# Two feed-forwards' gated results, turned by transposing DMAs of 16-bit words instead of TensorE transposes

## Chip, cores and metric

One core of a Trainium2 chip. The metric is the device time of one execution in microseconds (us). Engines in short: PE is TensorE, PEld its weight loads, DVE VectorE, ACT ScalarE, POOL GpSimd, SP SyncE (it issues most DMAs).

## What is computed

A decoder layer for 256 tokens of 2048 features, in float32. In the order of the program:

```
h = layer_norm(alpha * x + 0.5 * swiglu(x, w_ffn1_gu, w_ffn1_down))
h = layer_norm(alpha * h + mixers(h))          # retention and sliding-window attention, gated
h = layer_norm(alpha * h + 0.5 * swiglu(h, w_ffn2_gu, w_ffn2_down))
h = layer_norm(alpha * h + sigmoid(h @ w_ple_gate) * (p @ w_ple_proj))

def swiglu(x, w_gu, w_down):
    g, u = split(x @ w_gu, 2)                  # 2048 -> 2 x 5632
    return (silu(g) * u) @ w_down              # 5632 -> 2048
```

The change lies in `swiglu`, between the gate and the product with `w_down`, in both feed-forwards (f1 and f2).

## The kernel before

**Products.** Every float32 product is made of three faster ones: an operand is parted into a high half (rounded to fp32r, by ACT, line 98) and a low rest (by DVE, line 99), and `Sum.add` (lines 393 to 395) issues low x high, high x high and high x low into one PSUM bank. A matmul has 128 rows of tokens (two halves t = 0, 1) and up to 512 columns.

**Weights** come as chunks of 512 KB, loaded by SP (line 112) into buffers of one pool, `slots`, with 46 buffers of 4 KB per partition that all bigger tiles of the kernel share. A chunk is then parted by ACT and DVE. A plan lists all units of weights in the order in which they are used; `fill` (line 279) loads and parts units ahead of TensorE until some 45 matmuls are ready and some 90 loaded, as long as a budget of buffers allows. It is called whenever a unit is done, so the order on each engine's queue is fixed when the program is built, and every engine works through its queue in order.

There are four kinds of units. `Single` (P in the strings of line 873 ff.) is one chunk and 12 matmuls. `Folded` (F, line 147) is the same, but its low half is made by ACT (a negated copy, line 163) and an accumulating DMA that POOL issues (line 164) in place of DVE's subtraction; f1 uses four of them in a block. `Seven` (S) takes a pair of chunks and makes the four sub-products of a 2 x 2 block scheme with seven sums in place of eight; DVE makes sums of weights for it (lines 189 to 192). `Prepared` (D, f2 alone) is a Seven whose sums were made and stored earlier.

**A feed-forward** (`ffn`) goes through its 5632 columns of g and u in eleven blocks j of 512. In each, `block` (line 425) runs the units, which fill the banks `pg` and `pu` (and four more for the sevens). Then the sums are folded (lines 500 to 504, 993), ACT applies Silu (994 or 999), and DVE multiplies (995 or 1001): the result `v` has 128 tokens on the partitions, two halves of tokens and 512 features, in float32. For the second product the features must lie on the partitions, so `v` is turned: `turned(j, v)` (line 929). It takes two PSUM banks, lets TensorE transpose eight squares of 128 x 128 (line 937) and ACT copy the two banks into `raw` (line 939). `raw` is parted only when the blocks are through (`convert`, line 943), or used as it is for the sevens of the second product.

**What sets the place of the turn.** `side` is a list of jobs; behind every unit's matmuls `run_side` (line 329) takes the first one and calls it. `later(n, job)` (line 1130) puts a job behind n others. At the end of block j line 1002 asks for `later(2, turned)`, so the turn is issued behind the third unit of block j + 1, when `v` has long been ready. PSUM has eight banks, given out in turn.

The units of a block of f1 stand in the order F F S S F S S F, and each F counts two units of `run_side`, one for g and one for u.

Of the kernel before, what the change touches and what calls it, by code (L numbers as in the profile page):

```python
# [8 lines left out]
F32 = mybir.dt.float32  # L9
F32R = mybir.dt.float32r  # L10
I32 = mybir.dt.int32
AF = mybir.ActivationFunctionType
ALU = mybir.AluOpType
PSUM = bass.MemoryType.PSUM

P = 128
S = 256
# [38 lines left out]
def layer(ctx: ExitStack, tc: tile.TileContext, io):  # L56
    nc = tc.nc
    sync, act, dve, pool, pe = nc.sync, nc.scalar, nc.vector, nc.gpsimd, nc.tensor
# [8 lines left out]
    def bank(name):  # L67
        return psum.tile([P, 512], F32, tag="ps", name=name)

    def banks(name):  # L70
        return [bank(name + str(j)) for j in range(2)]

    def slot(shape, dt, name):
        return slots.tile(shape, dt, tag="slot", name=name)
# [477 lines left out]
    def rsqrt(dst, var, n, eps):  # L552
# [7 lines left out]
        )  # L560
        s = small.tile([P, n], I32, tag=f"ns{n}", name="ns", bufs=2)
        dve.tensor_scalar(s, v[:, 0].bitcast(I32), 1, None, ALU.logical_shift_right)
        y = small.tile([P, n], I32, tag=f"ny{n}", name="ny", bufs=2)
        dve.tensor_scalar(y, s, -1.0, float(0x5F3759DF - 2**31), ALU.mult, ALU.add)
# [37 lines left out]
    def ln_stats_by_root(stats, i, t, eps, between):  # L602
# [4 lines left out]
        root = small.tile([P, 1], F32, tag="nq1", name="nroot")  # L607
        act.activation(root, mv[:, 1:2], AF.Sqrt, bias=roots[eps], scale=4.0)
        v = small.tile([P, 1], F32, tag="nb1", name="nv")
# [10 lines left out]
    def table_of(f):  # L620

        act.activation(warm, warm, f)
# [16 lines left out]
    def ln_turn(y, t, i, new, k0, nk, keep=None):  # L639

        ps = bank(f"lnps{i}{t}{k0}").rearrange("p (a b) -> p a b", a=4)[:, :nk]
        for j in range(nk):
            k = k0 + j
            pe.transpose(ps[:, j, :], y[k // 4][:, t, k % 4 * P : (k % 4 + 1) * P], ident)
        if keep is not None:
            full = keep[:, k0 % 4 : k0 % 4 + nk, t * P : (t + 1) * P]
            act.copy(full, ps)
            ps = full
        dst = new[:, k0 : k0 + nk, :]
        split(dst[:, :, t * P : (t + 1) * P], dst[:, :, S + t * P : S + (t + 1) * P], ps)  # L650

    class Norm:
# [36 lines left out]
        def turn(self, t, c):  # L689

            args = self.y, t, self.i, self.new
            if c < 3 and (t, c + 1) != self.put_off:
                self.more(t, c + 1)
            self.sums_behind()
            if c == 0:
                for k0 in (0, 2):
                    ln_turn(*args, k0, 2, self.keep.get(c))
            else:
                ln_turn(*args, 4 * c, 4, self.keep.get(c))
# [19 lines left out]
        def run(self, steps, lhs, events, blks=(), calm=2):  # L719


            self.vectors = vectors.pop()
            table_of(AF.Sqrt)
            self.new = big.tile([P, KD, 512], F32R, tag="ht", name=f"ht{self.i}")
# [20 lines left out]
        def first(self, steps, lhs, sums, events):  # L745
# [14 lines left out]
            self.put_away()  # L760
            table_of(AF.Silu if self.i < 2 else AF.Sigmoid)

# [48 lines left out]
    ident = const.tile([P, P], F32, name="ident")  # L811
# [23 lines left out]
    def rotary_table(nm):  # L835

        inv, sgn = (0, 2) if nm == "r" else (1, 3)
        pos_i = slot([P, S], I32, "pos_i" + nm)
        act.dma_start(pos_i, io["positions"].broadcast_to([P, S]))
# [20 lines left out]
        yield  # L860
        act.activation(nb, n, AF.Sin)
        yield
# [5 lines left out]
        yield  # L868
        act.activation(cos, na, AF.Sin)
        yield  # L870
# [48 lines left out]
    def ffn(name, i, ht, norm, keep, residual, keepers, away):  # L919
# [3 lines left out]
        raws = []  # L923
# [4 lines left out]

        def turned(j, v):

            raw = slot([P, 4, S], F32, f"{name}a{j}")
            raws.append(raw)
            ps = banks(f"{name}t{j}")
            for k in range(4):
                for t in range(2):
                    at = slice(k % 2 * S + t * P, k % 2 * S + t * P + P)
                    pe.transpose(ps[k // 2][:, at], v[:, t, k * P : (k + 1) * P], ident)
            for h in range(2):
                act.copy(raw[:, 2 * h : 2 * h + 2], ps[h].rearrange("p (b n) -> p b n", b=2))

        acts = {}

# [5 lines left out]
        for j in range(KF // 4):  # L948
# [40 lines left out]
            if got:  # L989
                g, v = got  # L990
                for x, ps in ((g, pg), (v, pu)):
                    for t in range(2):
                        dve.tensor_tensor(x[:, t], x[:, t], ps[t], ALU.add)  # L993
                act.activation(g, g, AF.Silu)  # L994
                dve.tensor_tensor(v, g, v, ALU.mult)
            else:
                v = slot([P, 2, 512], F32, f"{name}v{j}")
                for t in range(2):
                    act.activation(v[:, t], pg[t], AF.Silu)
                for t in range(2):  # L1000
                    dve.tensor_tensor(v[:, t], v[:, t], pu[t], ALU.mult)
            later(2, lambda j=j, v=v: turned(j, v))
        stats = small.tile([P, 2, 4, 6], F32, tag="stats", name=name + "st", bufs=1)

        def others(n, ahead=45):
# [77 lines left out]
    def joined(ps, name, dst=None):  # L1083
        lo = half(name + "lo")
        v = half(name + "v") if dst is None else dst
        for f in range(2):
            act.copy(lo[:, f], ps[f][:, S:])
            dve.tensor_tensor(v[:, f], ps[f][:, :S], lo[:, f], ALU.add)
        return v
# [40 lines left out]
    def later(n, job):  # L1130
        for j in range(n):
            if len(side) <= j:
                side.append(idle)
        side.insert(n, job)
# [683 lines left out]
```

## Time and profile before

| | |
|---|---|
| median of 3 runs | 2269.6 us (2269.53 to 2271.87) |
| time of the profiled execution | 2269.44 us |
| its span, from first to last instruction | 2267.3 us |
| granted TensorE clock | 0.999 |
| matmuls and transposes on PE | 10482, 2258.9 us busy |
| DVE | 2576 instructions, 1975.9 us |
| ACT | 1543 instructions, 1272.5 us |
| DMA | 536.69 MB, mean 237 GB/s |

The span is 2 us shorter than the execution's time, which has a start and an end around it. Busy time is the union of an engine's instructions; matmuls overlap each other in the pipeline (0.39 us each, one started every 0.23 us), so PE can be busy all the time and still vary in pace. Times inside the trace are given from the start of the span. f1's blocks lie in about 10 to 478 us, f2's in about 1480 to 1945 us, the second products behind each. A row of a group gives line, engine, operation, tiles (written <- read), shapes, count, busy time and mean duration of one, and then the engine's idle time in front of them and what ended it. A row in time gives start, duration, and in square brackets the idle time just before.

### The profile page before, as it was taken

What the parts mean: (1) busy time and instruction counts of PE and PEld (TensorE: products, weight loads), DVE (VectorE), ACT (ScalarE), POOL (GpSimd) and SP (SyncE); (2) the same over time, 40 slices, a digit from 0 to 9 for tenths busy, and PEclk for the clock granted to TensorE, in tenths of its full rate; (3) what the DMA queues carried; (4) which work ended last, traced back from release to release, by engine and by line L of the source; (5) the groups of instructions that cost most, each with busy time, mean ns of one, the idle gap of its engine ahead of it and who ended that gap; (6) DMA issues with size and microseconds to landing.
All of it is one profiled execution on the core that took longest, in us unless ns stands there. A gap on an engine that the chain in (4) does not pass through costs nothing.

```text
span 2267.3 us, 29270 instructions
## 1 busy us (share of the span) xinstructions
PE 2258.9 (100%) x10482; PEld 1877.7 (83%) x10482; DVE 1975.9 (87%) x2576; ACT 1272.5 (56%) x1543; POOL 37.1 (2%) x49
## 2 busy tenths in 40 slices
PE   9999999999999999999999999999999999999998
PEld 7888888888888888888778888888888888888887
DVE  7988989999989887888789788689999999889887
ACT  6676776656555444535566454455555565555543
POOL 0000010000000000000000000000000000000000
PEclk9999999999999999999999999999999999999999
DMA  9888898865677878775456568787867766555772
GB/s 316 249 261 252 238 262 243 250 208 186 216 285 261 291 282 289 256 236 183 140 158 225 183 211 293 271 288 247 297 242 250 255 197 218 196 190 209 290 269 73
DMA packets 216889, 536.69 MB, mean 237 GB/s; under 512 B 17052, under 2 KB 21532, under 8 KB 216744
## 3 DMA queue, kind: packets, MB, share of 16 engines
q1 hardware_dynamic: 209000, 511.28, 65.9%
q0 software_dynamic: 5760, 20.97, 5.1%
q10 hardware_dynamic: 1984, 2.58, 0.4%
q8 instruction: 82, 1.34, 0.2%
q14 instruction: 63, 0.52, 0.1%
HBM read 484.43 MB, written 29.36 MB: 227 GB/s over the span
## 4 chain that ended last, share of the span: by engine, by line
PE 78%; DVE 1%; DMA 1%; ACT 0%; issue 0%; ACTq 0%; DVEq 0%
PE f2g L395 3%; PE f2g L393 3%; PE f2g L394 3%; PE rqk L344 3%; PE f2u L393 2%; PE f2u L395 2%; PE f2u L394 2%; PE aqk L344 2%; PE f1d L395 2%; PE f2d L394 2%; PE f2d L395 2%; PE f1d L393 2%; PE f1d L394 2%; PE f2d L393 2%; PE f1e L395 1%; PE f2e L394 1%
## 5 line engine op out<-in xcount | busy, mean ns | idle before, releaser
L99 DVE TENSOR_TENSOR lf_gu<-rf_gu,hf_gu 128x1024 fp32r<-128x1024 f32 (+1 forms) x229 | 271.9, 1210 | 11.1 <-ACT hf_gu L98 10.4
L98 ACT CAST hf_gu<-rf_gu 128x1024 fp32r<-128x1024 f32 (+1 forms) x229 | 232.8, 1041 | 30.2 <-DMA rf_gu<-in_f_gu 29.9
L99 DVE TENSOR_TENSOR lf_down<-rf_down,hf_down 128x1024 fp32r<-128x1024 f32 x150 | 178.8, 1220 | 19.0 <-ACT hf_down L98 18.5
L99 DVE TENSOR_TENSOR lw_in_f<-rw_in_f,hw_in_f 128x1024 fp32r<-128x1024 f32 x140 | 167.5, 1220 | 25.0 <-ACT hw_in_f L98 24.7
L98 ACT CAST hf_down<-rf_down 128x1024 fp32r<-128x1024 f32 x150 | 151.7, 1049 | 50.7 <-DMA rf_down<-in_f_down 18.0
L98 ACT CAST huf_gu<-uf_gu 128x1024 fp32r<-128x1024 f32 x75 | 79.0, 1053 | 147.5 <-DVE uf_gu L190 138.0
L98 ACT CAST hw_in_f<-rw_in_f 128x1024 fp32r<-128x1024 f32 x140 | 140.3, 1050 | 3.2 <-PE rv L394 1.4
L98 ACT CAST hvf_gu<-vf_gu 128x1024 fp32r<-128x1024 f32 x75 | 79.1, 1055 | 31.7 <-DVE vf_gu L192 30.8
L99 DVE TENSOR_TENSOR luf_gu<-uf_gu,huf_gu 128x1024 fp32r<-128x1024 f32 x75 | 91.4, 1219 | 0.0
L99 DVE TENSOR_TENSOR lvf_gu<-vf_gu,hvf_gu 128x1024 fp32r<-128x1024 f32 x75 | 91.4, 1218 | 0.0
L393 PE MATMUL f1g<-hf_gu,xt 128*128 128x512 f32 x232 | 90.6, 390 | 0.2 <-ACT hf_gu L98 0.2
L395 PE MATMUL f1g<-lf_gu,xt 128*128 128x512 f32 x232 | 90.7, 391 | 0.0
L394 PE MATMUL f1g<-hf_gu,xt 128*128 128x512 f32 x232 | 90.4, 390 | 0.0
L393 PE MATMUL f2g<-hf_gu,ht 128*128 128x512 f32 x217 | 84.7, 390 | 0.0
L395 PE MATMUL f2g<-lf_gu,ht 128*128 128x512 f32 x217 | 84.7, 390 | 0.0
L394 PE MATMUL f2g<-hf_gu,ht 128*128 128x512 f32 x217 | 84.5, 390 | 0.0
L994 ACT ACTIVATE eve<-eve 128x1024 f32<-128x1024 f32 x20 | 21.2, 1061 | 100.4 <-DVE eve L993 100.4
L395 PE MATMUL f1u<-lf_gu,xt 128*128 128x512 f32 x192 | 75.0, 390 | 0.7 <-DMA lf_gu<-rf_gu 0.7
L393 PE MATMUL f1u<-hf_gu,xt 128*128 128x512 f32 x192 | 75.7, 394 | 0.0
L394 PE MATMUL f1u<-hf_gu,xt 128*128 128x512 f32 x192 | 74.9, 390 | 0.0
L393 PE MATMUL f2u<-hf_gu,ht 128*128 128x512 f32 x172 | 68.2, 397 | 0.0
L395 PE MATMUL f2u<-lf_gu,ht 128*128 128x512 f32 x172 | 67.1, 390 | 0.0
(1468 smaller groups left out, 6734.7 us busy)
## 6 DMA issues: line engine op xcount, KB each, us to landing
rf_gu<-in_f_gu SPq DMA_DIRECT2D x360, 512.0 KB
rf_down<-in_f_down SPq DMA_DIRECT2D x176, 512.0 KB
rw_in_f<-in_w_in_f SPq DMA_DIRECT2D x148, 512.0 KB
lf_gu<-rf_gu POOLq DMA_DIRECT2D x40, 512.0 KB, 7.0
rw_rv<-in_w_rv SPq DMA_DIRECT2D x32, 512.0 KB
rw_ret<-in_w_ret SPq DMA_DIRECT2D x32, 512.0 KB
rw_mix<-in_w_mix SPq DMA_DIRECT2D x32, 512.0 KB
rw_pg<-in_w_pg SPq DMA_DIRECT2D x32, 512.0 KB
```

The source lines that it names most:

```text
L98: act.copy(dst_hi, src)
L99: (lo_engine or dve).tensor_tensor(dst_lo, src, dst_hi, ALU.subtract)
L344: pe.matmul(ps[f], hi[:, kk, f * P : (f + 1) * P], rhs(k), start=k == 0, stop=k == n_k - 1,)
L393: pe.matmul(o, al, bh, start=first, stop=False)
L394: pe.matmul(o, ah, bh, start=False, stop=False)
L395: pe.matmul(o, ah, bl, start=False, stop=self.left == 0)
L994: act.activation(g, g, AF.Silu)
```

## The change

`turned` no longer uses TensorE or PSUM. ACT copies the 16-bit words of `v` apart, all lower ones and all upper ones (`words`); one DMA on SP's queue transposes the sixteen squares of 128 x 128 words into `moved`; ACT copies these into `raw`, each word to its place. A float32 is thus moved as two words, bit for bit. `words` and `moved` are two buffers of the pool. The three steps are issued at different places: the copies apart behind the second unit of the next block (`later(1, ...)`), the DMA behind the third (`later(0, turn)`), the copies together behind the sixth (`later(3, joined)`).

```diff
+U16 = mybir.dt.uint16
...
         def turned(j, v):
-            raw = slot([P, 4, S], F32, f"{name}a{j}")
-            raws.append(raw)
-            ps = banks(f"{name}t{j}")
-            for k in range(4):
-                for t in range(2):
-                    at = slice(k % 2 * S + t * P, k % 2 * S + t * P + P)
-                    pe.transpose(ps[k // 2][:, at], v[:, t, k * P : (k + 1) * P], ident)
+            words = slot([P, 2, 2, 512], U16, f"{name}w{j}")
+            of_v = v.bitcast(U16).rearrange("p t (n h) -> p h t n", h=2)
             for h in range(2):
-                act.copy(raw[:, 2 * h : 2 * h + 2], ps[h].rearrange("p (b n) -> p b n", b=2))
+                act.copy(words[:, h], of_v[:, h])
+            moved = slot([P, 2, 2, 4, P], U16, f"{name}m{j}")
+
+            def turn():
+                sync.dma_start_transpose(
+                    moved.rearrange("p h t k n -> p (h t k) n"), words.rearrange("p h t n -> p (h t n)")
+                )
+
+            def joined():
+                raw = slot([P, 4, S], F32, f"{name}a{j}")
+                raws.append(raw)
+                of_raw = raw.bitcast(U16).rearrange("p k (t n h) -> p h t k n", t=2, h=2)
+                for h in range(2):
+                    act.copy(of_raw[:, h], moved[:, h])
+
+            later(0, turn)
+            later(3, joined)
...
-            later(2, lambda j=j, v=v: turned(j, v))
+            later(1, lambda j=j, v=v: turned(j, v))
```

In the built program PE has 176 transposes fewer, ACT 44 copies of 128 x 1024 words each way in place of 44 of 128 x 512 out of PSUM, and SP 22 DMAs more. The order of everything else is the same, but the buffers that tiles get are other ones, and with them what some loads wait for.

## Prediction

> **What bounds the kernel now.** I read the page first, then the waits of TensorE, then the busy time by stretch, and at last the order in time around one of the 22 places where the change cuts.
>
> ```profile
> span 2267.3 us, 29270 instructions
> ...
> PE 2258.9 (100%) x10482; PEld 1877.7 (83%) x10482; DVE 1975.9 (87%) x2576; ACT 1272.5 (56%) x1543; POOL 37.1 (2%) x49
> ...
> q1 hardware_dynamic: 209000, 511.28, 65.9%
> q0 software_dynamic: 5760, 20.97, 5.1%
> q10 hardware_dynamic: 1984, 2.58, 0.4%
> ```
>
> ```profile
> PE warm L1697 <- POOL ident masks.py:199: 1.4, 1, 1.4
> PE f1u L395 <- DMA lf_gu<-rf_gu: 0.7, 1, 0.7
> ```
>
> TensorE is busy for the whole span, and the longest things it ever waited for are 1.4 us at the start and, once, 0.7 us for an accumulating DMA of the first feed-forward. A busy PE could still be a slow one, so the cadence matters:
>
> ```profile
> 99.20 0.39 PE L394 MATMUL f1g<-hf_gu,xt 128*128 128x512 f32 x1
> 99.42 0.40 PE L395 MATMUL f1g<-lf_gu,xt 128*128 128x512 f32 x1
> 99.66 1.04 PE L937 MATMUL f1t<-ident,evw 128*128 128x128 f32 x8
> 100.45 0.48 PE L393 MATMUL f1u<-hf_gu,xt 128*128 128x512 f32 x1
> 100.77 0.40 PE L394 MATMUL f1u<-hf_gu,xt 128*128 128x512 f32 x1
> 101.00 0.39 PE L395 MATMUL f1u<-lf_gu,xt 128*128 128x512 f32 x1
> ```
>
> Matmuls start every 0.23 us (100.77 to 101.00), one behind the other. So the kernel is bound by the number of TensorE instructions, and whatever leaves TensorE without making it wait is gained in full. The second question is how much room the others have:
>
> ```profile
> 91.50:133.20 41.70, 41.70 (x189) 34.64 (x188) 37.53 (x46) 28.47 (x33) 3.47 (x4) 1.00 0.84 250
> 133.20:174.90 41.70, 41.70 (x189) 34.64 (x188) 37.60 (x46) 28.50 (x33) 3.44 (x4) 1.00 0.85 247
> 1520.00:1945.00 425.00, 425.00 (x1921) 353.11 (x1920) 400.01 (x470) 241.03 (x279) 0.00 (x0) 1.00 0.71 241
> ```
>
> The first two rows are blocks j = 2 and 3 of the first feed-forward (f1), the third the eleven blocks of the second (f2), 38.6 us each. Behind the length stand PE, PEld, DVE, ACT, POOL, the granted clock, the DMA share and GB/s. DVE has 4.1 us free in a block of f1, ACT 13.2, the DMA engines 15% or 6.3 us. In f2 the DMA engines have 29%, 11.2 us a block.
>
> **The change part by part.**
>
> *TensorE loses 176 transposes.*
>
> ```profile
> L937 PE MATMUL f1t<-ident,evw x80: 271/273/273, 99.7 to 476.9; 128*128 128x128 f32 x80
> L937 PE MATMUL f2t<-ident,evw x80: 271/273/273, 1568.7 to 1942.0; 128*128 128x128 f32 x80
> L937 PE MATMUL f1t<-ident,f1v x8: 271/272/273, 58.0 to 58.7; 128*128 128x128 f32 x8
> L937 PE MATMUL f2t<-ident,f2v x8: 270/273/273, 1527.6 to 1528.4; 128*128 128x128 f32 x8
> ```
>
> That is 22 groups of eight. From the matmul at 99.42 to the second one behind the group at 100.77 it is 1.35 us; without the group it is two steps of 0.227, 0.45 us. A group costs 0.90 us, 22 of them **19.7 us**. All of it is on the path, since TensorE never rests.
>
> *ScalarE: two copies out, four in.*
>
> ```profile
> L939 ACT COPY f1a<-f1t x22: 572/586/592, 61.1 to 477.2; 128x512 f32<-128x512 f32 x22
> L939 ACT COPY f2a<-f2t x22: 573/587/596, 1528.3 to 1942.4; 128x512 f32<-128x512 f32 x22
> ```
>
> ```profile
> L98 ACT CAST hf_gu<-rf_gu 128x1024 fp32r<-128x1024 f32 x61 | 63.8, 1045 | 0.0
> ```
>
> The four new copies move 1024 two-byte words per partition, each with a stride of two words on one side. No row has such a form. They might take 0.5 us (twice as fast for half the bytes) or 2.1 us (twice as slow for the stride); I take the cast's 1.05 us, the nearest row of the same count. Per turn ACT gains 4 x 1.05 - 2 x 0.59 = 3.0 us, and 28.5 becomes 31.5 us of a block of 41 us. Whether that is hidden depends on the place:
>
> ```profile
> 96.40 1.06 ACT L98 CAST hvf_gu<-vf_gu 128x1024 fp32r<-128x1024 f32 x1 [0.40 <-DVE vf_gu L192]
> 97.36 1.04 ACT L98 CAST hf_gu<-rf_gu 128x1024 fp32r<-128x1024 f32 x1
> 101.67 1.06 ACT L98 CAST huf_gu<-uf_gu 128x1024 fp32r<-128x1024 f32 x1 [2.75 <-DVE uf_gu L190]
> 104.02 1.07 ACT L939 COPY f1a<-f1t 128x512 f32<-128x512 f32 x2
> 110.86 1.05 ACT L98 CAST hvf_gu<-vf_gu 128x1024 fp32r<-128x1024 f32 x1 [0.38 <-DVE vf_gu L192]
> 111.82 1.05 ACT L98 CAST hf_gu<-rf_gu 128x1024 fp32r<-128x1024 f32 x1
> 116.08 1.06 ACT L98 CAST huf_gu<-uf_gu 128x1024 fp32r<-128x1024 f32 x1 [2.69 <-DVE uf_gu L190]
> ```
>
> In the built order the two parting copies come behind the first of these casts, at 97.4, and end at 99.5. The casts behind them slide into the 2.75 us that ACT idled before 101.67. The two joining copies come behind the cast that ends at 111.9 and fill the 2.69 us idle before 116.08. In between, the two copies at 104.02 go. So ACT's additions cost nothing, and what follows 104.02 is one microsecond earlier. If the stride doubles the price, parting ends at 101.6 and the next cast at 102.7; DVE wants it at 102.95, so even that about fits.
>
> *SP: one more issue, and a wait.* The transposing DMA stands in the built order of SP behind the load that was issued at 89.21. It waits for the parting copies, 99.5.
>
> ```profile
> 89.21 1.61 SPq L112 DMA_DIRECT2D rf_gu<-in_f_gu  x2
> 94.18 0.88 SPq L112 DMA_DIRECT2D rf_gu<-in_f_gu  x2
> 103.46 0.37 SPq L112 DMA_DIRECT2D rf_gu<-in_f_gu  x1
> ```
>
> ```profile
> 114.75 0.69 DVE L189 TENSOR_TENSOR uf_gu<-rf_gu,rf_gu 128x512 f32<-128x512 f32 x1
> ```
>
> Queued behind it are the second load of the first row, which went out before 91, and the two from 94.18; the next one left at 103.46 anyway. They lose up to 9 us. The first two are wanted by ACT at 111.82 (with the joining copies, 113.9) and by DVE at 114.75. Issued from 99.5 on, behind a transposition that takes T, and needing some 5 us to land (the accumulating DMAs of the same size, below, needed 4.9 at least), they are in time while T stays under about 9 us. ACT reaches the joining copies at 111.9, so there the DMA itself may last 12.4 us from 99.5. Past that, ACT stands still with the casts of all weights behind it. The accumulating DMAs, whose results TensorE reads, are the tightest spot:
>
> ```profile
> 108.36 0.86 POOL L164 DMA_DIRECT2D lf_gu<-rf_gu  x1 [21.47 <-PE f1g L395]
> ```
>
> ```profile
> 115.97 0.40 PE L395 MATMUL f1u<-lf_gu,xt 128*128 128x512 f32 x1
> ```
>
> ```profile
> DMA to landing us min/median/max: 4.9/6.6/10.3
> ```
>
> Issued at 108.36 and used at 115.97: 7.6 us for something that takes 6.6 in the middle and 10.3 at worst. This one is issued 1 us earlier (104.02 above) and used 0.9 us earlier, a draw. The last one of a block is not issued earlier but used 0.9 us earlier; the one wait of 0.7 us in the table says that some have no slack. I put 3 us in all for f1: 0.9 us at two or three blocks, the rest for transfers that now run beside the transposition.
>
> *The DMA itself.* No transposing DMA is in this trace, so its engine time has to be bounded. 512 KB moved as a weight load: 65.9% of 16 engines for 511 MB is 0.659 x 2267.3 x 0.524 / 511.28 = 1.5 us. The accumulating DMA, also from SBUF to SBUF: 0.051 x 2267.3 / 40 = 2.9 us. By packets: q1's take 0.659 x 16 x 2267.3 us / 209000 = 114 ns for 2446 bytes on average, q10's 73 ns for 1300, so roughly 26 ns a packet and 0.036 ns a byte. In pieces of 256 bytes (128 two-byte words of a row) it would be 2048 x 35 / 16 = 4.5 us, in pieces of 32 bytes 16384 x 27 / 16 = 28 us. Less than the load's 1.5 has no reason. I take 3 to 4.5 us, next to the one row that is SBUF to SBUF; that is inside the 6.3 us free in f1 and far inside f2's 11.2.
>
> The page "DMA: Bandwidth & Descriptors" of the Trainium skill (Latency and other measured facts) gives 261 GB/s for a transposing DMA, an estimated 2.0 us for this one; the sum would stay the same. No run here shows it.
>
> *What is nowhere on the path.* Two PSUM banks a block fall away; no wait of TensorE in the list above is for a bank. The words and the moved words take two more buffers, for some 15 us each; loads that wait for a buffer may shift by a few us, which I leave in the range.
>
> **Sum.** 2269.4 (the profiled execution's own time; the median of the three runs is 2269.6, so nothing to correct) - 19.7 + 3 = **2253 us**, 0.7% faster. What this measurement can tell from no change is about 0.2%, 4.5 us.
>
> **The rivals.**
>
> *The pieces are small (slower).* The place is the DMA engines in f1; it decides from 6.3 us of engine time per transposition, and with f2's 9.9 us gain to lose, the total turns slower from about 7.2. Between 4.5 and 28 I take the middle by ratio, 11.2 us: f1 then lasts 11 x (11.2 - 6.3) = 54 us longer than now, f2 just fits and keeps its 9.9, 2269.4 + 54 - 9.9 = 2313 us. At 28 us it would be 2269.4 + 11 x 21.7 + 11 x 16.8 = 2693. For it: two-byte elements, and a share of 0.84 already. Against it: nothing that the trace shows.
>
> *The blocks go one after another (slower).* The DMA holds sixteen squares of 128 x 128 words. If each were issued like a load (0.44 us, by the two in 0.88 us above) that is 7 us, if each ran its course alone (4.9 us) 78. The middle by ratio is 23 us; ACT is then stuck for 23 - 12.4 in each of 22 turns, 2269.4 - 19.7 + 233 = 2483 us. The Trainium skill, "VectorE: DVE Perf Modes" (The three transpose paths), gives 1309 ns for one such square by DMA against 390 ns on TensorE. Sixteen in a row are an estimated 20.9 us, and this sum would be 2437. On TensorE this trace has 273 ns, and 99 ns from one to the next, so the page's figures for squares taken singly need not hold in a row.
>
> *The accumulating DMAs eat f1's gain.* Their slack is near nothing, and every block moves 0.5 MB more. f1 stays as it is, f2 gains: 2259.5 us.
>
> *DVE takes over.* 37.5 of 41.7 us are busy, and the chain of a block begins with TensorE's last sums:
>
> ```profile
> 125.33 0.69 DVE L501 TENSOR_TENSOR evw<-eve,f12s 128x512 f32<-128x512 f32 x1 [1.50 <-PE f12s L395]
> 130.02 1.37 DVE L993 TENSOR_TENSOR eve<-eve,f1g 128x512 f32<-128x512 f32 x2 [0.75 <-PE f1g L395]
> 132.74 1.37 DVE L993 TENSOR_TENSOR evw<-evw,f1u 128x512 f32<-128x512 f32 x2 [1.35 <-PE f1u L395]
> ```
>
> But its idle time, 1.50 + 0.75 + 1.35, is all waiting for TensorE and more than 0.9. If DVE were the bound after all, nothing would be gained: 2268.
>
> **How the numbers follow.** Forecast 0.50 (its own range 2248 to 2260), f1's gain lost 0.10, DVE 0.06, small pieces 0.25, one after another 0.09. The range begins at 2247, under the full 19.7 (2249.7) by what two banks fewer may give. To leave out no more than 0.2 it must take in the cheaper 0.15 of the small pieces, to 2330. Faster by over 0.2%: 0.50 + 0.10 = 0.60. Within: 0.06 and 0.01 of the small pieces, 0.07. Slower: 0.33.
>
> **What would show it.** The L937 groups gone and TensorE's steps of 0.23 us unbroken through the place, its waits still under a few us, blocks of f1 of 40.8 us: right. TensorE waiting for lf_gu by DMA in every block of f1: the accumulating DMAs. ACT idle before the joining copies with a DMA as releaser, or SP idle behind the transposing DMA: one of the slow rivals, told apart by the DMA share in f1 (towards 1.0 for small pieces, unchanged for blocks one after another). The time from issue to landing of the transposing DMA decides everything: under 9 us the forecast stands.

## The result, and the profile after

| | before | after |
|---|---|---|
| median | 2269.84 us (6 runs) | 2261.84 us (6 runs, 2261.55 to 2263.47) |
| ratio, 95% interval | | 0.9965 [0.9953, 0.9977] |
| profiled execution, its span | 2269.44, 2267.3 us | 2261.55, 2259.8 us |

The kernel is 8.0 us faster. The forecast was 16.4 us (2253): the direction came out right, but a little under half of the gain came. The stated range, 2247 to 2330, holds the measured time; it was that wide for the sake of the slow rivals. Line numbers of the changed kernel are one higher than before (matmuls 394 to 396, casts 99, subtractions 100, loads 113, accumulating DMAs 165); the parting copies are line 936, the transposing DMA 940, the joining copies 949.

The page of the changed kernel, first lines and DMA part:

```profile
span 2259.8 us, 29055 instructions
...
PE 2244.9 (99%) x10306; PEld 1856.8 (82%) x10306; DVE 1975.7 (87%) x2576; ACT 1345.9 (60%) x1587; POOL 37.1 (2%) x49
...
DMA packets 262649, 548.22 MB, mean 243 GB/s; under 512 B 62812, under 2 KB 67292, under 8 KB 262504
...
q1 hardware_dynamic: 254760, 522.82, 68.5%
```

The 176 transposes are gone (10482 to 10306). PE is busy 14.0 us less, but the span shrank by only 7.5: what PE stands idle grew from 8.4 to 14.9 us. A matmul's record lasts 0.39 us and the next one starts 0.23 us behind it, so a delay of up to some 0.16 us (an estimate from these two) leaves no idle time; the waits listed below can therefore be less than what was lost. Before, 17052 packets were under 512 bytes; now 45760 more are, 2080 for each of 22 transpositions, which for 512 KB are pieces of 256 bytes.

The new operations (line, engine, operation, tiles, count: shortest/median/longest ns, first and last start):

```profile
L936 ACT COPY f2w<-evw x20: 1036/1042/1048, 1558.9 to 1933.6; 128x1024 uint16<-128x1024 uint16 x20
...
L949 ACT COPY f1a<-f1m x22: 1342/1352/1366, 69.4 to 481.6; 128x1024 uint16<-128x1024 uint16 x22
L949 ACT COPY f2a<-f2m x22: 1333/1352/1368, 1535.3 to 1944.6; 128x1024 uint16<-128x1024 uint16 x22
...
L940 SPq DMA_TRANSPOSE f1m<-f1w x11: 1323/1920/3397, 56.9 to 468.7; - x11
L940 SPq DMA_TRANSPOSE f2m<-f2w x11: 1323/1894/3316, 1520.4 to 1934.7; - x11
```

Parting costs 1.04 us a copy, joining 1.35, and SP's issue 1.3 to 3.4 us.

**Where the time came from.** Three stages can be dated by the first matmul of the product behind each: `rv`, the first product behind f1; `f2g`, the first of f2; `pg`, the first behind f2. First and last start stand behind the durations. Before:

```profile
L393 PE MATMUL rv<-hw_rv,ht x128: 388/390/478, 706.2 to 884.3; 128*128 128x512 f32 x128
L393 PE MATMUL f2g<-hf_gu,ht x217: 388/390/482, 1473.1 to 1929.7; 128*128 128x512 f32 x109
L393 PE MATMUL pg<-hw_pg,ht x128: 388/390/481, 2165.4 to 2254.7; 128*128 128x512 f32 x128
```

After:

```profile
L394 PE MATMUL rv<-hw_rv,ht x128: 389/389/478, 699.8 to 877.9; 128*128 128x512 f32 x128
L394 PE MATMUL f2g<-hf_gu,ht x217: 387/389/478, 1466.5 to 1922.2; 128*128 128x512 f32 x109
L394 PE MATMUL pg<-hw_pg,ht x128: 389/389/499, 2157.3 to 2247.1; 128*128 128x512 f32 x128
```

Eleven turns of 0.90 us are 9.9 us in each feed-forward. f1 gained 706.2 - 699.8 = **6.4 us**. f2, from `f2g` to `pg`, took 692.3 us and now takes 690.8: **1.5 us**. So f1 loses 3.5 of its 9.9, and f2 8.4. These two numbers, "f1 gain" and "f2 gain", are given for every experiment below, each from its own three rows. They come from one profiled execution. Six kernels of this study run f1 as the changed kernel does, and gained 6.4, 7.6, 6.3, 7.2, 6.1 and 7.2 us there: a single value is good to about 0.8 us. This is the scatter between kernels that have the same turn in f1; between kernels with other copies or buffers there it may be larger.

**Who waits now.** TensorE's longest waits (us in total, times, longest):

```profile
PE f1u L396 <- DMA lf_gu<-rf_gu: 2.9, 5, 1.0
PE warm L1710 <- POOL ident masks.py:199: 1.4, 1, 1.4
PE f26s L396 <- DVE luf_gu L100: 0.8, 1, 0.8
PE f28s L396 <- DVE luf_gu L100: 0.8, 1, 0.8
PE f27s L396 <- DVE luf_gu L100: 0.8, 1, 0.8
PE f25s L396 <- DVE luf_gu L100: 0.5, 1, 0.5
```

In f1 it is the accumulating DMAs, 2.9 us where it was 0.7. In f2, where TensorE had not waited once, there are now twelve rows, 4.5 us in all. The four longest are shown: in the blocks 5 to 8 it waits for `luf_gu`, the low half of a sum of weights that DVE makes for the sevens. That is also where f2's loss lies. If a block's stretch ends with the last matmul of its sevens, the stretches were, in us, and behind the comma DVE's busy time in them:

| stretch of block | 2, 3, 4, each | 5 | 6 | 7 | 8 | 5 to 8 |
|---|---|---|---|---|---|---|
| before | 41.0 | 41.1, 38.1 | 41.7, 40.3 | 41.0, 36.5 | 41.7, 41.1 | 165.5 |
| the change | 40.1 to 40.2 | 41.3, 35.6 | 42.9, 42.3 | 42.1, 35.9 | 42.8, 42.2 | 169.1 |
| no_dma (below) | 40.1 to 40.2 | 40.1, 36.0 | 42.7, 42.2 | 40.1, 38.9 | 40.8, 40.2 | 163.7 |
| far_f2 (below) | 40.1 to 40.2 | 40.2, 36.5 | 42.2, 41.6 | 40.1, 38.8 | 40.8, 40.1 | 163.3 |

The blocks 2 to 4 gain 0.8 to 0.9 us each. The blocks 5 to 8 should gain 3.6 and lose 3.6, 7.2 of the 8.4 us. The profile's rows of these four (columns as in the prediction):

```profile
1665.70:1707.00 41.30, 40.65 (x178) 33.05 (x177) 35.56 (x43) 24.55 (x28) 0.00 (x0) 1.00 0.82 285
1707.00:1749.90 42.90, 41.71 (x182) 33.60 (x181) 42.31 (x50) 30.21 (x34) 0.00 (x0) 1.00 0.79 250
1749.90:1792.00 42.10, 40.99 (x179) 32.99 (x178) 35.91 (x44) 23.09 (x27) 0.00 (x0) 1.00 0.75 262
1792.00:1834.80 42.80, 41.62 (x181) 33.51 (x180) 42.21 (x50) 30.13 (x34) 0.00 (x0) 1.00 0.79 244
```

In the stretches 5 and 7 DVE stands idle for 5.7 and 6.2 us; in 6 and 8 it is busy all but 0.6 us, and the block goes at DVE's pace. So what DVE misses in one block TensorE waits for in the next. Without the DMA (no_dma) that is left once: 4.1 us idle in stretch 5, 0.5 in 6.

One long stretch of each feed-forward, f1 and then f2:

```profile
100.00:470.00 370.00, 366.95 (x1612) 301.81 (x1611) 339.39 (x407) 286.69 (x305) 29.56 (x35) 1.00 0.93 264
1515.00:1930.00 415.00, 410.69 (x1797) 335.97 (x1796) 392.21 (x461) 266.57 (x291) 0.00 (x0) 1.00 0.76 251
```

DVE is busy 392 of 415 us in f2, so it has little to make up for what it receives late. And SP, f1 at the place that the prediction looked at, in order of time:

```profile
87.73 2.90 SPq L113 DMA_DIRECT2D rf_gu<-in_f_gu  x2
98.14 1.91 SPq L940 DMA_TRANSPOSE f1m<-f1w  x1
100.15 7.67 SPq L113 DMA_DIRECT2D rf_gu<-in_f_gu  x5
```

For 7.5 us (90.63 to 98.14) nothing was issued, and then five loads follow in a row. SP's waits ahead of the transposing DMA in f2:

```profile
SPq L940 <- ACT hf_gu L99: 34.9, 3, 15.5
SPq L940 <- ACT bf_gu L99: 34.6, 6, 8.9
SPq L940 <- PE f2g L395: 14.4, 3, 8.7
SPq L940 <- PE f2u L396: 8.1, 1, 8.1
```

ScalarE as the releaser (by the casts close behind the parting copies) is read as the wait for the words (wait_only, below, names them); TensorE is the wait for a buffer, as SP has it in front of its loads too.

### The profile page after: what moved, and what is told of

Same layout as the page of the kernel before. It is cut to its first block, busy times and chain, and to the rows that moved or that the text cites. A ratio compares the mean times of both kernels' runs of the same rounds, so it can differ in the third digit from the quotient of the medians.

```text
span 2259.8 us, 29055 instructions
## 1 busy us (share of the span) xinstructions
PE 2244.9 (99%) x10306; PEld 1856.8 (82%) x10306; DVE 1975.7 (87%) x2576; ACT 1345.9 (60%) x1587; POOL 37.1 (2%) x49
## 3 DMA queue, kind: packets, MB, share of 16 engines
q1 hardware_dynamic: 254760, 522.82, 68.5%
## 4 chain that ended last, share of the span: by engine, by line
PE 89%; DVE 4%; DMA 4%; issue 3%; ACT 0%; ACTq 0%; POOL 0%; POOLq 0%; DVEq 0%
PE rqk L345 3%; PE f2g L396 2%; PE f2g L395 2%; PE f2g L394 2%; PE f1g L394 2%; PE f1g L396 2%; PE f1g L395 2%; PE f1u L396 2%; PE f2u L396 2%; PE f2u L395 2%; PE f2u L394 2%; DMA lf_gu<-rf_gu 2%; PE f1u L394 2%; PE f1u L395 2%; PE aqk L345 2%
## 5 line engine op out<-in xcount | busy, mean ns | idle before, releaser
L100 DVE TENSOR_TENSOR lf_down<-rf_down,hf_down 128x1024 fp32r<-128x1024 f32 x150 | 178.8, 1219 | 19.7 <-ACT hf_down L99 17.5
```

What stands on the lines that cost most here:

```text
L100: (lo_engine or dve).tensor_tensor(dst_lo, src, dst_hi, ALU.subtract)
```

## The experiments

The theory after the result: the transposition itself is quick and ScalarE's copies are hidden, but the transposing DMA on SP's queue makes weight loads late, by its wait, its traffic or its buffers, and in f2 DVE passes that on to TensorE. Rivals: ScalarE's copies delay the casts; or the transposes were hidden in part and there was never more to gain. In the expectations L is late loads, C ScalarE's copies and B the two buffers; from wait_only to reuse the letters are new: A is SP's wait, B the traffic, C the extra buffer. All ratios are against the kernel before on the same chip; its medians there lie between 2269.5 and 2270.3 us, so that a difference between runs of two chips holds up to 0.8 us of that; "lf_gu" is TensorE's total wait for accumulating DMAs in f1 (0.7 before).

| run | median us | ratio, 95% interval | f1 gain | f2 gain | lf_gu |
|---|---|---|---|---|---|
| the change | 2261.84 | 0.9965 [0.9953, 0.9977] | 6.4 | 1.5 | 2.9 |
| no_turn | 2255.24 | 0.9941 [0.9927, 0.9954] | 5.8 | 8.1 | 4.0 |
| only_f1 | 2262.02 | 0.9967 [0.9954, 0.9979] | 7.6 | 0.1 | 1.6 |
| only_f2 | 2268.94 | 0.9994 [0.9986, 1.0003] | -0.7 | 0.7 | 0.8 |
| act_queue | 2300.61 | 1.0139 [1.0125, 1.0152] | -25.7 | -4.7 | 25.0 |
| late_turn | 2265.82 | 0.9981 [0.9973, 0.999] | 3.8 | 0.0 | 3.7 |
| no_dma | 2253.28 | 0.9923 [0.991, 0.9937] | 9.7 | 7.1 | 0.7 |
| no_join | 2261.5 | 0.996 [0.9947, 0.9972] | 3.7 | 3.6 | 4.3 |
| two_less | 2267.26 | 0.9986 [0.9977, 0.9995] | 6.3 | -3.4 | 3.1 |
| wait_only | 2259.49 | 0.9954 [0.9942, 0.9967] | 4.1 | 5.8 | 4.9 |
| traffic_only | 2255.44 | 0.9936 [0.9923, 0.995] | 9.2 | 4.9 | 1.4 |
| plain_copy | 2257.84 | 0.9945 [0.9932, 0.9957] | 8.2 | 3.9 | 1.3 |
| reuse | 2264.67 | 0.9976 [0.9967, 0.9986] | 3.8 | 0.6 | 4.7 |
| late_both | 2273.77 | 1.0015 [1.0007, 1.0024] | -4.1 | 1.4 | 12.1 |
| late_both3 | 2269.06 | 1.0 [0.9992, 1.0009] | 0.1 | 4.0 | 6.0 |
| late_far | 2265.84 | 0.9983 [0.9972, 0.9993] | -15.3 | 7.8 | 17.8 |
| far_f2 | 2255.27 | 0.9937 [0.9923, 0.9951] | 7.2 | 8.1 | 2.4 |
| far_f2_8 | 2255.57 | 0.9938 [0.9925, 0.9951] | 6.1 | 6.2 | 3.0 |
| far_room34 | 2253.37 | 0.9928 [0.9914, 0.9942] | 7.2 | 9.2 | 2.7 |

### Which half loses, and how much there was to gain

**no_turn**, against the kernel before (features are not turned):

```diff
-            ps = banks(f"{name}t{j}")
...
-                    pe.transpose(ps[k // 2][:, at], v[:, t, k * P : (k + 1) * P], ident)
...
-                act.copy(raw[:, 2 * h : 2 * h + 2], ps[h].rearrange("p (b n) -> p b n", b=2))
+                act.copy(raw[:, 2 * h : 2 * h + 2], v[:, h].rearrange("p (b n) -> p b n", b=2))
```

> Nothing is turned at all: the transposes are gone and ACT copies v into raw as it stands, so the feed-forwards multiply the wrong numbers; it shows what TensorE's 176 transposes cost when nothing takes their place. If each group of eight is worth its 0.90 us everywhere: 2269.8 - 19.7 = 2250 us, f2 faster by 9.9. If VectorE bounds f2's blocks whatever the turn costs: f2 gains some 2 to 4 us, in all 2256 to 2258 us, with TensorE waiting for VectorE's luf and lvf in f2 as in the changed kernel.

**only_f1** and **only_f2**: one feed-forward by DMA, the other by TensorE as before.

```diff
-            later(1, lambda j=j, v=v: turned(j, v))
+            if name == "f1":
+                later(1, lambda j=j, v=v: turned_dma(j, v))
+            else:
+                later(2, lambda j=j, v=v: turned_pe(j, v))
```

> The first feed-forward turns by DMA, the second on TensorE as before. The traces of before and after, matmul by matmul, put 6.1 us of the gain into f1's blocks and 1.9 into f2's. If the two are independent: 2263.5 us. If f1's DMA turns hurt something later (buffers shifted for the rest of the program): slower than that.

> The second feed-forward turns by DMA, the first on TensorE. Independent: 2268 us, with TensorE's waits for luf and lvf in f2's blocks 5 to 8 as in the changed kernel. If the buffers left over from f1 had caused the waits in f2: 2260 us, f2's full 9.9 us.

Measured: no_turn 2255.24, so 14.8 us are there when nothing is transposed, between the two times expected. It does not reach 19.7: f2 gains 8.1 of 9.9, and f1 only 5.8, with 4.0 us of waits for accumulating DMAs although nothing is transposed. That the missing part was never there to gain is ruled out for f1 by no_dma below (9.7). only_f1 gains what the whole change gains, only_f2 nothing that can be told from zero. The greater loss is f2's.

### ScalarE's copies

**no_dma** parts and joins in the same places, but nothing is moved between:

```diff
-            moved = slot([P, 2, 2, 4, P], U16, f"{name}m{j}")
-            def turn():
-                sync.dma_start_transpose(
...
-                    act.copy(of_raw[:, h], moved[:, h])
+                    act.copy(of_raw[:, h], words[:, h].rearrange("p t (k n) -> p t k n", k=4))
-            later(0, turn)
```

> No DMA turns anything: ACT parts the words and joins them again in the same places, so what is multiplied is not turned; the buffer of the moved words is gone too. Theory L: f2 gains 8 us as without any turn, in all 2255 us. Theory C: 2262 us, as in the changed kernel. Theory B: in between, as one of the two buffers is gone, about 2258.

**no_join** keeps the DMA and joins by two plain copies of `v` (its features are not turned):

```diff
-                    act.copy(of_raw[:, h], moved[:, h])
+                    act.copy(raw[:, 2 * h : 2 * h + 2], v[:, h].rearrange("p (b n) -> p b n", b=2))
```

> ACT parts the words and the DMA transposes them, but the joining copies (2 x 1.35 us) are replaced by two copies of 128 x 512 out of v (0.59 us each in the kernel before), so nothing turned is multiplied. Theory L: 2262 us, as in the changed kernel. Theory C: about 2257 us, less the parting copies' share. Theory B: 2262.

Measured: 2253.28 with all four copies and no DMA, the forecast's own time; 2261.5 with the DMA and without the strided joining, the change's. In the whole time ScalarE's copies cost nothing that shows, and the DMA costs 2261.84 - 2253.28 = 8.6 us. By stages no_join is less clear: f2 gains 2.1 us more than in the change and f1 2.7 less. And no_turn, with fewer copies than no_dma, is 2.0 us slower, by f1: differences of this size come with any other arrangement of copies and buffers, and their cause is open. The rows of no_dma that date its stages:

```profile
L394 PE MATMUL rv<-hw_rv,ht x128: 389/389/478, 696.5 to 874.6; 128*128 128x512 f32 x128
...
L394 PE MATMUL f2g<-hf_gu,ht x217: 389/389/478, 1463.2 to 1913.5; 128*128 128x512 f32 x109
...
L394 PE MATMUL pg<-hw_pg,ht x128: 389/389/481, 2148.4 to 2237.7; 128*128 128x512 f32 x128
```

and its busy time in the stretches shown above:

```profile
100.00:470.00 370.00, 369.30 (x1629) 305.20 (x1628) 342.60 (x415) 287.26 (x305) 29.56 (x35) 1.00 0.87 253
1515.00:1930.00 415.00, 413.75 (x1820) 341.07 (x1820) 396.81 (x466) 271.43 (x296) 0.00 (x0) 1.00 0.71 243
```

f1 keeps 9.7 of 9.9 us and f2 7.1. So of f2's 8.4 us of loss 2.8 are there without the DMA, and 5.6 come with it. The DMA shares give what a transposition takes of the 16 engines: nine start in the first stretch, (0.93 - 0.87) x 370 / 9 = 2.5 us; ten in the second, (0.76 - 0.71) x 415 / 10 = 2.1 us. The packet time of queue q1, 65.9% of 2250.2 us in no_dma and 68.5% of 2259.8 in the change, gives 3.0 us for each of 22.

### Another queue, another place, fewer buffers

**act_queue** lets ScalarE issue the DMA right behind its copies:

```diff
-                sync.dma_start_transpose(
+                act.dma_start_transpose(
```

> The transposing DMA is issued by ACT, behind its own parting copies, so SP never waits for them and the weight loads keep their times. If the loads held back on SP's queue (77.5 us of SP waiting in 13 turns) cause the waits of f1 and f2: about 2255 us. If ACT's own time is what hurts (the joining copies, 1.35 us each, and now the issue of 1.3 to 3.4 us on top): 2262 us or more.

Measured: 2300.61, far worse, which neither expectation foresaw in size. SP waits for no words any more (ScalarE waits twice for moved ones, 9.2 and 3.2 us), and its loads wait for the transposing DMA itself five times, 35.3 us in all (once, 1.0 us, in the change). TensorE waits for the accumulating DMAs:

```profile
PE f1u L396 <- DMA lf_gu<-rf_gu: 25.0, 7, 5.5
```

**late_turn** moves the DMA alone one unit back, which shortens its distance to the joining copies:

```diff
-            later(0, turn)
+            later(1, turn)
```

> The transposing DMA is issued one unit later, the copies stay in their places, so SP holds back the weight loads for a shorter time while it waits for the parting copies. Theory L (f2's lost 6.6 us come from weight loads that are late because SP waits and the DMA engines carry more): f2 gains some 5 us more than the changed kernel, in all about 2257 us. Theory C (from ACT's four long copies, which push back casts that VectorE waits for): unchanged, 2262 us. Theory B (from the two extra buffers, for which VectorE or loads wait): unchanged, 2262.

**two_less** takes two buffers from the budget for weights:

```diff
-AHEAD_SLOTS = 32
+AHEAD_SLOTS = 30
...
-                slots_for_weights(24)
+                slots_for_weights(22)
```

> f2's blocks plan their weights with two buffers less (22 and 30 in place of 24 and 32), which makes up for words and moved. Theory B: VectorE no longer waits for buffers in f2, about 2257 us. Theories L and C: 2262 us, or slower by what weights prepared less far ahead cost.

Measured: 2265.82 and 2267.26, both slower than the change: two_less by f2 (4.9 us), late_turn by f1 (2.6) and f2 (1.5). Theory L had expected 2257 of late_turn, and that was missed; on SP's queue its DMA passes two loads in a block of f1, and in f2 none in most blocks. DVE's waits for loads there, first in late_turn, then in two_less:

```profile
DVE uf_gu L190 <- DMA rf_gu<-in_f_gu: 12.6, 3, 6.2
```

```profile
DVE uf_gu L190 <- DMA rf_gu<-in_f_gu: 15.1, 4, 5.6
```

It is 4.7 us in the changed kernel, and 5.1 more that TensorE ended. The kernel before had such waits too, at the same two places (stretches 5 and 7), and TensorE none behind them:

```profile
DVE uf_gu L189 <- DMA rf_gu<-in_f_gu: 6.3, 2, 3.9
```

That points to late loads in f2. Why the DMA makes them late was still open: wait, traffic or buffer.

### The DMA taken apart

**wait_only** (nothing turned): SP waits as before, and then moves 32 bytes per partition.

```diff
-                sync.dma_start_transpose(
-                    moved.rearrange("p h t k n -> p (h t k) n"), words.rearrange("p h t n -> p (h t n)")
-                )
+                sync.dma_start(moved[:, 0, 0, 0, :16], words[:, 0, 0, :16])
...
-                    act.copy(of_raw[:, h], moved[:, h])
+                    act.copy(of_raw[:, h], words[:, h].rearrange("p t (k n) -> p t k n", k=4))
```

> In place of the transposing DMA, SP issues at the same spot a DMA of 32 bytes per partition from the words to the moved buffer; ScalarE joins from the words, so the activations are not turned. SP waits for the parting copies as before and the extra buffer is held, but almost nothing is moved. Theory A (SP stands still at the wait, and the loads queued behind it go out late): as slow as the changed kernel, 2261 to 2263 us. Theory B (the traffic of the transposition delays loads and accumulating DMAs): as fast as the kernel without that DMA, 2253 to 2255 us. Theory C (the extra buffer makes loads wait): 2259 to 2262 us.

**traffic_only** (nothing turned): the whole transposition, of something that is there already.

```diff
-                    moved.rearrange("p h t k n -> p (h t k) n"), words.rearrange("p h t n -> p (h t n)")
+                    moved.rearrange("p h t k n -> p (h t k) n"), ht[:, 0:2, :].bitcast(U16).rearrange("p h n -> p (h n)")
...
-                    act.copy(of_raw[:, h], moved[:, h])
+                    act.copy(of_raw[:, h], words[:, h].rearrange("p t (k n) -> p t k n", k=4))
```

> The transposing DMA stays at its spot with the same size and the same destination, but reads a part of the layer's input that has long been there, so SP does not wait for the parting copies; ScalarE joins from the words, so the activations are not turned. Theory A (SP's wait): 2253 to 2256 us. Theory B (the traffic): 2260 to 2263 us. Theory C (the extra buffer): 2259 to 2262 us, as in the run with the wait alone.

**plain_copy** (nothing turned): the same 512 KB as a plain DMA.

```diff
-                sync.dma_start_transpose(
-                    moved.rearrange("p h t k n -> p (h t k) n"), words.rearrange("p h t n -> p (h t n)")
-                )
+                sync.dma_start(moved.rearrange("p h t k n -> p (h t k n)"), words.rearrange("p h t n -> p (h t n)"))
```

> The transposing DMA becomes a plain one of the same 512 KB between the same two buffers, at the same spot, with ScalarE joining from its result; the activations are not turned. Theory B in its narrow form (the 256-byte pieces of the transposition are what hurts): 2255 to 2258 us. Theory A, C, or any traffic of that size: 2260 to 2263 us.

**reuse**: the transposition writes into `v`'s buffer, the joining into the words'; a turn takes no more buffers than before the change.

```diff
-            moved = slot([P, 2, 2, 4, P], U16, f"{name}m{j}")
+            moved = v.bitcast(U16).rearrange("p t (h k n) -> p t h k n", h=2, k=4)
...
-                raw = slot([P, 4, S], F32, f"{name}a{j}")
+                raw = words.rearrange("p h t n -> p (h t n)").bitcast(F32).rearrange("p (k s) -> p k s", k=4)
```

> The changed kernel without its additional buffers: the transposing DMA writes into the buffer of v, which the parting copies have read by then, and ScalarE joins into the buffer of the words. A turn then holds two buffers instead of three, and no buffer is asked for at the joining. Theory C (the extra buffer): 2255 to 2259 us, with fewer waits of VectorE for loads in the second feed-forward. Theories A and B: 2261 to 2263 us, unchanged.

Measured: 2259.49, 2255.44, 2257.84 and 2264.67. In wait_only the profile names the words as what SP waits for:

```profile
SPq L940 <- ACT f2w L936: 57.7, 9, 12.9
```

The wait alone costs 6.2 us against no_dma, the traffic alone 2.2; with no wait for the words 6.4 of the 8.6 us come back. That the turn's own buffers are the cause is not borne out: with the buffers given back it is 2.8 us slower. By stages it is less simple than the sums say. In f1 the wait alone cost 5.6 us (9.7 - 4.1) and the traffic alone 0.5. In f2 each alone cost little, 1.3 and 2.2 us, and both together 5.6 (7.1 - 1.5): what is late twice is past its slack, which is argued from these numbers and not shown. plain_copy does not fit SP's wait alone: with the same wait, the same bytes and the same place it is 4.0 us faster than the change, in the band expected if the small pieces hurt, and even faster than wait_only. It differs from the change in two things, far fewer packets (3168 more than before in 22 turns, not 45760) and an issue that holds SP for 0.47 us, not 1.3 to 3.4. No run tells these two apart; traffic_only has both, with issues of 1.8 to 6.3 us, and lost only 2.2, so neither costs much without the wait. Why reuse loses in f1 is open too.

SP still waits in traffic_only, but for buffers (the three longest groups):

```profile
SPq L940 <- PE f2g L396: 25.4, 5, 9.2
SPq L940 <- PE f2u L396: 18.6, 3, 7.2
SPq L940 <- PE f1u L396: 17.1, 5, 5.2
```

A wait for a buffer seems to cost little here, presumably since a load in its place would have had one too (argued, not shown); the wait for the words is an additional one.

### The remedy: past the loads

If the wait costs because loads stand behind it, the DMA must go behind these loads, and the joining as much later.

```diff
-            later(0, turn)
-            later(3, joined)
+            later(2, turn)
+            later(5, joined)
```

**late_both** is this edit, **late_both3** has 3 and 6, **late_far** 3 and 6 in f1, 6 and 9 in f2.

> The whole computation. The transposing DMA is issued two units later and the joining copies two units later, so the distance between them stays as in the changed kernel. On SP's queue the DMA of a block of the first feed-forward moves behind three loads; in the second mostly none. If SP's standing wait for the words is what delays loads, the first feed-forward gains back up to the 9.2 us of the run with the traffic alone (2.7 more than the changed kernel) and the second stays: 2259 us. If the place does not matter: 2262 us. If the joining is late instead: 2264 us or more.

> As the run before, but three units later each: the transposing DMA passes four loads in the first feed-forward and five in the second. SP's wait as the cause: both feed-forwards gain, 2256 to 2258 us. The place not mattering: 2262 us. The words' buffer, held longer, as a new cause: the second feed-forward loses, 2264 us or more.

> As the run before in the first feed-forward; in the second the transposing DMA and the joining come six and nine units later than the parting, behind ten loads. SP's wait as the cause: 2256 to 2258 us, no wait of SP for the words left in the second. The buffers as the cause: the second feed-forward loses against the run before, since two buffers are held for half a block more.

Measured: 2273.77, 2269.06 and 2265.84, none better than the change, and none what SP's wait alone would have given. The halves go apart. In f2 the gain grows with the loads passed, counted on SP's queue in the traces, in the middle one of the eleven blocks: 1.4 us with three, 4.0 with five, 7.8 with ten, where the change has 1.5 with none. (late_both passes none to six, so the expectation's "mostly none" was not so.) In f1 it vanishes, through the accumulating DMAs; TensorE's waits in late_both, late_both3 and late_far:

```profile
PE f1u L396 <- DMA lf_gu<-rf_gu: 12.1, 10, 3.3
```

```profile
PE f1u L396 <- DMA lf_gu<-rf_gu: 6.0, 6, 1.8
```

```profile
PE f1u L396 <- DMA lf_gu<-rf_gu: 17.8, 7, 7.6
```

The expectation that f1 would gain back up to 9.2 us was wrong. Why the place behind three or four loads is bad there is not shown; ScalarE does not wait for the moved words in any of the three. What is seen is that SP's issue of the transposing DMA lasts longer in f1, 4.5 us in the middle in late_both and 3.7 in late_both3 against 1.9. late_far's executions lie between 2260.7 and 2276.7 us and the profiled one is the longest, so its f1 value says only that f1 is far off.

So: f1 as the changed kernel has it, and only f2 later.

```diff
-            later(0, turn)
-            later(3, joined)
+            later(0 if name == "f1" else 6, turn)
+            later(3 if name == "f1" else 9, joined)
```

**far_f2** is this, **far_f2_8** has 8 and 11, and **far_room34** adds `AHEAD_SLOTS = 34`, two more buffers for weights in f2.

> The whole computation. The first feed-forward is as in the changed kernel; in the second the transposing DMA comes six and the joining nine units after the parting, behind ten loads on SP's queue. If SP's standing wait is what cost the second its gain, and the first feed-forward's losses of the last runs belong to the accumulating DMAs alone, the second gains 6 to 7 us more than in the changed kernel: 2255 to 2257 us. If the gain of the second in the last run was a chance of that execution, or came from the slower first: 2262 us.

> The same with eight and eleven units. SP's wait as the cause and already gone at six: 2255 to 2257 us, as the run before. The buffers, held longer, as a second cost: 2258 us or more.

> As far_f2, with a budget of weight buffers two larger in the second feed-forward (AHEAD_SLOTS 34 in place of 32), so that loads are issued earlier. If the buffers that words and moved words hold are what is left of the loss: 2253 to 2255 us. If nothing is left to gain there: 2255 to 2257 us, as far_f2. If the pool has no more to give and the loads wait for others' buffers: slower than far_f2.

Measured: 2255.27, 2255.57 and **2253.37**. All compute the whole layer, and all beat both kernels; far_room34 is 16.1 us faster than before, and its interval [0.9914, 0.9942] lies below the change's. No run gives the kernel before the larger budget, so how much of that is the turn's stays open. What SP waits for ahead of the DMA in f2 in far_f2:

```profile
SPq L940 <- PE f2g L396: 21.6, 4, 7.9
SPq L940 <- DVE lf_gu L100: 15.0, 2, 8.6
SPq L940 <- PE f22s L396: 7.6, 1, 7.6
```

ScalarE is no longer among the releasers: the words lie ready, and f2 gains 8.1 of 9.9 us. This is so although SP's issue of the DMA lasts longer there, 1.7 to 9.9 us, and the traffic is the same; the joining copies went along, and what they did is not told apart. The delay can be followed down the line. DVE's first sum of a pair of weights in f2, with its idle time behind the last bar, in the changed kernel and then in far_f2:

```profile
L190 DVE TENSOR_TENSOR uf_gu<-rf_gu,rf_gu 128x512 f32<-128x512 f32 x35 | 23.9, 684 | 9.8 <-PE f2g L396 5.1 <-DMA rf_gu<-in_f_gu 4.7
```

```profile
L190 DVE TENSOR_TENSOR uf_gu<-rf_gu,rf_gu 128x512 f32<-128x512 f32 x35 | 23.9, 683 | 0.8 <-DMA rf_gu<-in_f_gu 0.8
```

DVE's 9.8 us of idle time there, 4.7 ended by a load and 5.1 by TensorE, became 0.8, and TensorE's twelve waits for DVE in f2 became two, 0.8 us in all. Before the change it had been 6.3, with no wait of TensorE; in the shorter blocks there is presumably less room for such a wait. The larger budget of far_room34 is worth 1.9 us more in the median, little more than these runs tell apart; far_f2_8 shows nothing further to gain from a still later place.

## Why the prediction was right and wrong

**TensorE's 19.7 us: right.** no_dma, with the transposes gone and everything else in place but the DMA, gains 9.7 of 9.9 us in f1 and 7.1 in f2. Of the 2.8 us missing in f2, some two lie in the stretch of block 6, which goes at DVE's pace (42.7 us, DVE busy 42.2).

**ScalarE: right, with one price off.** Parting was put at 1.05 us and took 1.04; joining took 1.35 instead of 1.05. It still fits: in the changed kernel the joining copies follow a cast without a gap, and the next one (the 2.69 us of idle time that the prediction filled) has 0.26 us left.

```profile
110.63 2.58 ACT L949 COPY f1a<-f1m 128x1024 uint16<-128x1024 uint16 x2
113.08 1.04 ACT L99 CAST hf_gu<-rf_gu 128x1024 fp32r<-128x1024 f32 x1
114.02 0.61 ACT L99 CAST bf_gu<-rf_gu 128x512 fp32r<-128x512 f32 x1
114.89 1.05 ACT L99 CAST huf_gu<-uf_gu 128x1024 fp32r<-128x1024 f32 x1 [0.26 <-DVE uf_gu L191]
```

**The DMA's engine time: a little high, and rightly no bound.** It took 2.1 to 3.0 us against 3 to 4.5, in pieces of 256 bytes as in the cheaper bound. The rivals of small pieces and of blocks one after another, a third of the chance, did not happen. The profile lists no landing for this DMA, but the joining copies, 12.5 us behind its issue in the turn shown (110.63 against 98.14), did not wait for it in any turn. The Trainium skill's figure in "VectorE: DVE Perf Modes" (The three transpose paths), 1309 ns for a square, does not add up over sixteen squares in one DMA: that would be an estimated 20.9 us. The Trainium skill's page "DMA: Bandwidth & Descriptors" (Latency and other measured facts) gives 261 GB/s for a non-contiguous case, an estimated 2.0 us; the trace's 2.1 to 3.0 is near it.

**f1's loss: right in size, in part by luck.** 3 us were allowed, 3.5 were lost (2.3 to 3.8 in six runs), and the waits are where the prediction put them, at the accumulating DMAs. But it counted transfers beside the transposition, and the traffic alone lost 0.7 us in f1, the wait alone 5.8; and no_turn lost 4.1 there with no DMA at all. The rival that they eat the whole of f1's gain came near the measured time, 2259.5, with the losses in the wrong half.

**f2's loss: the step that failed.** The prediction found that the loads behind the transposing DMA "lose up to 9 us" and weighed this at one place, in f1, against what DVE and ScalarE want there. For f2 it asked only whether the DMA engines have room ("far inside f2's 11.2"), and counted the 9.9 us in full: the sum has no term for a loss in f2. Measured are 8.4 us of loss, 5.6 by the DMA at this place and 2.8 without it. f2's DMA engines do have room; its late loads do not, since DVE, busy 400 of 425 us, catches up only at the cost of TensorE. The row was in the prediction, and it was read for the throughput instead of for the slack; it also gave f2's blocks 38.6 us each, by dividing by eleven a stretch that holds about ten, where the blocks 2 to 10 take 41.0 to 42.4. The bound that should have decided was taken from one place too: "under 9 us the forecast stands" was worked out for two loads of one block of f1, from the time of the transposition alone. ScalarE never waited for the moved words. Late were the weights queued behind the DMA, which waits for the words; how the loss divides between that wait, the issue and the packets is not settled for f2.

**Buffers: left in the range, and not seen as a cause.** Giving them back (reuse) did not help; two fewer for the weights cost 5.4 us (two_less), so the budget does matter, but nothing shows that the change paid for the turn's own buffers.

**The rival of DVE** had the right engine in f2 and only part of the reason: over f2 as a whole DVE has the throughput for most of the gain (no_dma and far_f2 gain 7.1 and 8.1 of 9.9), but single blocks go at its pace once it has stood idle in the block before (the stretches 6 and 8 above). No run relieves DVE, so this last step rests on the traces.

## What to carry to other kernels

A DMA that waits for a result is better not issued on the queue that carries the loads until that result is nearly there: count every load behind it, in each stage in which it stands, against the slack of the engine that parts the weights, not against that engine's or the DMA's free share. The place can differ by stage: ten loads later was worth 6.6 us in f2, while three loads later in f1 came with longer waits for the accumulating DMAs and cost more than the change had gained. An experiment that keeps the wait without the traffic, and one that keeps the traffic without the wait, are a good first cut, but they need not add up: in f2 each alone cost 1.3 and 2.2 us and both together 5.6, and only moving the DMA showed what the place was worth.

## What the hardware showed unexpectedly

- A transposing DMA of 512 KB between two places of SBUF takes 2.1 to 3.0 us of the sixteen DMA engines, about as much as the accumulating DMA of the same size (2.9 us), but SP is held by its issue: 1.3 to 3.4 us in the changed kernel, 1.7 to 9.9 in f2 of far_f2, where a plain DMA of the same bytes at the same place (plain_copy) holds it 0.47 us.
- ScalarE's copy of 1024 two-byte words with a stride of two words costs 1.04 us when the stride is in what it reads and 1.35 us when it is in what it writes; a cast of as many four-byte words costs 1.05 us.
- The same DMA issued from ScalarE's queue instead of SP's made the kernel 38.8 us slower, with 25.0 us of TensorE's time in waits for accumulating DMAs. Why it disturbs those so much more is open.
